# A hybrid decoder layer on one core: another order of the opening loads, the key norm behind the values, the 32×32 inverse spread over partitions, output rows in bonus tiles

## The chip, the cores and the metric

One core of a Trainium2 chip runs the whole layer. The metric is the device time of a run in microseconds; lower is better. The engines are called as in the profile: PE (TensorE), DVE (VectorE), ACT (ScalarE), POOL (GpSimd) and SP (SyncE, which here only issues DMAs).

## The reference

One layer with three branches on x of 2048 tokens by 1024 channels, in float32, beside a memory of 256 tokens:

```
h   = rms_norm(x, g);  parts of h @ w_in feed the branches and their gates
A   = RWKV-7 time mixing, 8 heads of 64 (per head a 64x64 state, delta rule)
B   = sliding-window attention, 8 query and 2 key heads of 64, window 128, sinks
kv  = rms_norm(mem, gm) @ w_mem_kv;  km = rms_norm(kv[:, :512] per head);  vm = kv[:, 512:]
C   = softmax(rms_norm(q) km') vm, 4 heads of 128 over 256 memory tokens
out = x + (sum over branches of sigmoid(gate) * ((branch * silu(z)) @ w_proj)) @ w_out
```

In chunks of 64 tokens the delta rule of branch A needs, per head and chunk, the inverse of a unit triangular 64×64 matrix.

## The kernel before

The tokens go in four blocks of 512 (`TB`; `sb` is the block). All activations are kept transposed, channels on partitions. A float32 product is made of three `float32r` matmuls on split operands, high·high, high·low and low·high (`gemm3`, L501 to L507). Every weight is split into a high and a low part: ACT copies (L487), DVE subtracts (L488). In block 0 this is done on arrival, and the split pair is stored to DRAM (`k…`, L491); blocks 1 to 3 load the pair back as one 512 KB tile `whl` (L483). `whl` has six buffers, the raw weights `raw` three.

**The opening** (L383 to L423, L1353 on). The SP queue carries the loads in the order in which they are listed: transposed memory `memt` (four tiles `g`) and key weights `w_mk` (four tiles `big`), the identity, memory rows (`yl`), rows of x (`rt`, `g`), value weights `w_mv` (four `big` tiles; the last two stand behind x's columns), x's columns `in_xt` (`ya`, `yh`). `mem_split` makes the two parts of the normed memory (tiles `mB`). `mem_kv` (L638) then makes for each of four heads the keys (24 matmuls of 256 columns; weights split at L476 and L477), their sums of squares, the pow on POOL, two transposes that spread the scale over partitions, the scaled and split key, and its store to DRAM (`Kd`). Values follow (48 matmuls of 512 columns, L684 to L686) into two PSUM banks, `oo` and `as_`. The row scales of the memory (`mem_scales`) come first of all. `x_scales` and `x_cols` (L1338) then make block 0's input `hT` (`hH`, `hL`; L1347 to L1350) from x's rows and columns, and the first projection starts.

**A block.** Two streams are woven: branch A (`stream_r`) and branches C and B with their projections (`stream_f`). In branch A, `rwkv_prep` (L735) makes for a pair of heads the tiles QE, QO, AB, BK, and copies the 32×32 diagonal pieces of AB into `Nc` on ACT (L819 to L821). After two pairs, `rwkv_inverse` (L853) inverts all 64 pieces (4 partition groups × 16) at once: 32 partitions hold one piece's rows. In step s of 31, a stream shuffle on DVE (L863) spreads row s of every piece to its 32 partitions, a multiply (L864) and an add (L865) update the columns behind s of all of `Y`, 128 partitions × 16·(31−s) columns. Then a transposition on DVE (L868) and two groups of small PE products (L880, L888) make the lower left quarter of the 64×64 inverse, and `put` stores the result to DRAM (`fb`), from where `rwkv_chain` loads it. There are two inverses per block, eight in all. Carried columns of the token shift are copied at L714.

**The end of a block.** Branch A's last projection merges into the accumulators, and `output` (L1294) multiplies by `w_out`, in two halves of 512 channels: 96 matmuls into four PSUM banks (two of `mm`, two of `as_`), and then for each of the four row tiles a buffer of the pool `g` (L1306), its load of x's rows, the add on DVE, and the store, load and store on ACT's DMA queue:

```python
                xr = g2()
                nc.scalar.dma_start(xr, A["x"][rows, n * 512:(n + 1) * 512])
                V.scalar_tensor_tensor(xr, op[tt], 0.5, xr, op0=ALU.mult, op1=ALU.add)
                nc.scalar.dma_start(A["out"][rows, n * 512:(n + 1) * 512], xr)
```

The pool `g` has 11 buffers for everything short-lived. `ya`, `yh` and `yl` have four each: `ya` holds, for each pair of heads, the bonus term and then branch A's output, until it has been split for the projection.

**The order of the work.** The program is listed in one piece and then laid out anew by a list scheduler (`Step`, `lay_out`, `order`, L55 to L314): each instruction has a cost by engine, and each engine takes the ready instruction that was listed first, as buffers allow. The result is the fixed order of each engine; at run time an engine takes its instructions in that order and waits by semaphores. A DMA is laid out with 2200 ns, one on a tensor parked in DRAM (`fq`, `fb`, `fv`) with 4200 (`cost_SP`, L142). In the names, `g_…`, `k_…` and the like are tiles with their numbers.

Of the kernel before, what the change touches and what calls it, by code (L numbers as in the profile page):

```python
# [20 lines left out]
TB = 512  # L21
# [38 lines left out]
class Step:  # L60
# [256 lines left out]
def build(tc, A, nsb=4):  # L317
# [52 lines left out]
    def const(name, shape, src=None):  # L370
        t = (bp if name == "ident" else fp if name == "eye32" else cp).tile(shape, F32, name="c_" + name)
        nc.sync.dma_start(t, A[name] if src is None else src)
        return t
# [18 lines left out]

    def mk(h):
        early(rp.tile([128, 2, 512], F32, name="big", bufs=BIG), A["w_mk"][h].rearrange("p (b c) -> p b c", b=2), raws)
# [4 lines left out]
    for u in range(2):  # L399
        early(g2(shape=(128, 2, M)), A["memt"][256 * u:256 * (u + 1)].rearrange("(k p) t -> p k t", p=128), memt)  # L400
    mk(0)
    for u in range(2, 4):
        early(g2(shape=(128, 2, M)), A["memt"][256 * u:256 * (u + 1)].rearrange("(k p) t -> p k t", p=128), memt)
    mk(1)
    ident = const("ident", [128, 128])
    for i in range(2):
        for u in range(2):
            early(yrow("yl"), A["mem"][i * 128:(i + 1) * 128, u * 512:(u + 1) * 512], mem0)
    mk(2)
    for i in range(3):  # L410
        for u in range(2):
# [6 lines left out]
    for u in range(2):  # L418
        early(g2(), A["x"][384:512, u * 512:(u + 1) * 512], x0)
    mv(0)  # L420
    mv(1)
    for k in range(8):
        early(yrow("ya" if k < 4 else "yh"), A["xt"][k * 128:(k + 1) * 128, :TB], xt0)  # L423
# [175 lines left out]
    Kd = [dp.tile([128, 2, M], F32, name=f"mk{h}") for h in range(4)]  # L599
# [38 lines left out]
    def mem_kv(mT, ms, mr):  # L638
        kgs, sts = {}, {}

        def keys(h):
            o = mm_ps()[:, :M]
            gemm3(o, [(w, (mT[0][k], mT[1][k])) for k, w in enumerate(wtiles(None, 8, raw=raws[h]))])
            sq = g2()[:, :M]
            S.activation(sq, o, AF.Square)
            kg = g2()[:, :M]
            S.activation(kg, o, AF.Copy, scale=dcol("xg"))
            kgs[h] = sq, kg

        def stats(h):  # L650
            st = s_ps()
            tok_stat(kgs[h][0], 1, 2, st)
            rs = xp.tile([128, 8], F32, name="st8", bufs=2)
            V.scalar_tensor_tensor(rs[:, :2], st[:, :2], 1.0 / 128, ms, op0=ALU.mult, op1=ALU.add)
            G.tensor_tensor(rs[:, :2], rs[:, :2], mhalf[:, :2], op=ALU.pow)
            sts[h] = rs

        def scaled(h):
            kg = kgs[h][1]
            bc = s_ps()  # L660
            bcast_T(bc, sts[h], 1, 2)
            V.tensor_tensor(kg, kg, bc[:, :M], op=ALU.mult)
            km = rp.tile([128, 2, M], F32R, name="km", bufs=2)
            S.activation(km[:, 0], kg, AF.Copy)
            V.tensor_tensor(km[:, 1], kg, km[:, 0].bitcast(F32), op=ALU.subtract)
            nc.sync.dma_start(Kd[h], km.bitcast(F32))

        o = [o_ps(), s_ps()]
        for h in range(6):
            if h < 4:  # L670
                keys(h)
                yield 3.921
            if 1 <= h < 5:
                stats(h - 1)
            if h >= 2:
                scaled(h - 2)
            yield 1.796
            if h < 4:
                continue
            for k in range(4 * h - 16, 4 * h - 12):  # L680
                wh, wl = two_parts(raws[4 + k // 2][:, k % 2])
                for i in range(2):
                    sl = slice(i * 128, (i + 1) * 128)
                    PE.matmul(o[i], mT[0][k][:, sl], wh, start=k == 0, stop=False)  # L684
                    PE.matmul(o[i], mT[0][k][:, sl], wl, start=False, stop=False)
                    PE.matmul(o[i], mT[1][k][:, sl], wh, start=False, stop=k == 7)  # L686
# [9 lines left out]
        yield 9.836  # L696
# [20 lines left out]
    def tmp(tag="rt", bufs=NRT):  # L717
        return rp.tile([128, TB], F32, name=tag, bufs=bufs)

# [15 lines left out]
    def rwkv_prep(p, i, parks, dk, Pls, Nc, sb, hT, lwla, group):  # L735
# [83 lines left out]
        for q in range(4):  # L819
            qs = slice(32 * q, 32 * q + 32)  # L820
            S.activation(Nc[qs, i], AB[qs, :, 32 * (q % 2):32 * (q % 2) + 32], AF.Copy)  # L821
# [31 lines left out]
    def rwkv_inverse(group, parks, Nc):  # L853
# [3 lines left out]
        N_ = Nc.rearrange("p i c t -> p (i c) t")  # L857
        Y = rp.tile([128, n, 32], F32, name="Yi")
        V.tensor_copy(Y, eye32.unsqueeze(1).to_broadcast([128, n, 32]))
        for s in range(31):  # L860
            w = 31 - s
            bc = rp.tile([128, n, 32], F32, name="ibc", bufs=2)
            V.stream_shuffle(bc[:, :, :w], N_[:, :, s + 1:], [s] * 32)  # L863
            V.tensor_tensor(bc[:, :, :w], bc[:, :, :w], Y[:, :, s:s + 1].to_broadcast([128, n, w]), op=ALU.mult)  # L864
# [649 lines left out]
```

## Time and profile before

| | before |
|---|---|
| median of 3 runs | 2163.45 us (2163.43 to 2164.69) |
| profiled execution | 2162.26 us |
| its span, mean granted clock | 2160.5 us, 0.998 |
| PE / DVE / ACT / POOL busy | 2132.1 / 1556.2 / 830.3 / 131.9 us |
| DMA | 511.87 MB, 237 GB/s on average |

The span is the stretch in which the profile shows instructions; the execution's own time is 1.8 us longer. Busy time of PE is that of matmuls whose ends are modelled, so 99% says that PE had matmuls under way, not at what pace: the pace is read from the distance of their starts. PE's weight loads (PEld) run beside them. A group's row gives line, engine, operation, tiles with their shapes, and count; then busy time, mean ns of one, and the idle time of that engine ahead of them with what ended it.

### The profile page before, as it was taken

What the parts mean: (1) busy time and instruction counts of PE and PEld (TensorE: products, weight loads), DVE (VectorE), ACT (ScalarE), POOL (GpSimd) and SP (SyncE); (2) the same over time, 40 slices, a digit from 0 to 9 for tenths busy, and PEclk for the clock granted to TensorE, in tenths of its full rate; (3) what the DMA queues carried; (4) which work ended last, traced back from release to release, by engine and by line L of the source; (5) the groups of instructions that cost most, each with busy time, mean ns of one, the idle gap of its engine ahead of it and who ended that gap; (6) DMA issues with size and microseconds to landing.
All of it is one profiled execution on the core that took longest, in us unless ns stands there. A gap on an engine that the chain in (4) does not pass through costs nothing.

```text
span 2160.5 us, 37816 instructions
## 1 busy us (share of the span) xinstructions
PE 2132.1 (99%) x14260; PEld 1757.0 (81%) x14260; DVE 1556.2 (72%) x3731; ACT 830.3 (38%) x1757; POOL 131.9 (6%) x159
## 2 busy tenths in 40 slices
PE   8999999999999999999999999999999999999999
PEld 6888787777788888878888888887888888887887
DVE  7799999567578979754627988955455798894532
ACT  6655554336244353303414344421522434431220
POOL 2001000001000000001000100000100000000100
PEclk9999999999999999999999999999999999999999
DMA  9988787978866566585876656676676655758556
GB/s 324 333 273 266 256 280 236 345 272 307 322 231 206 181 211 203 182 293 179 279 260 208 197 185 205 207 250 212 230 259 233 208 184 194 225 173 288 184 193 204
DMA packets 254758, 511.87 MB, mean 237 GB/s; under 512 B 38256, under 2 KB 120432, under 8 KB 254576
## 3 DMA queue, kind: packets, MB, share of 16 engines
q1 hardware_dynamic: 238448, 480.08, 66.8%
q10 hardware_dynamic: 16128, 29.37, 4.1%
q8 instruction: 113, 1.85, 0.3%
q14 instruction: 69, 0.57, 0.1%
HBM read 375.67 MB, written 133.69 MB: 236 GB/s over the span
## 4 chain that ended last, share of the span: by engine, by line
PE 82%; DVE 8%; DMA 6%; issue 1%; ACT 1%; SPq 0%; POOL 0%; ACTq 0%; DVEq 0%; POOLq 0%
PE mm L507 20%; PE mm L505 20%; PE mm L506 20%; DVE whl L488 2%; DMA rt<-in_x 1%; DMA k<-whl 1%; PE mm L1303 1%; PE mm L1301 1%; PE mm L1302 1%; PE rw L983 1%; PE rw L966 1%; PE oo L1250 1%; PE rw L806 1%; DVE ibc L863 1%; PE rw L826 1%
## 5 line engine op out<-in xcount | busy, mean ns | idle before, releaser
L505 PE MATMUL mm<-hH,whl 128*128 128x512 f32 x1888 | 746.0, 395 | 2.9 <-DVE carry L714 2.8
L506 PE MATMUL mm<-hL,whl 128*128 128x512 f32 x1888 | 743.5, 394 | 1.5 <-DVE hL L1350 1.4
L507 PE MATMUL mm<-hH,whl 128*128 128x512 f32 x1888 | 744.6, 394 | 0.0
L505 PEld LDWEIGHTS mm<-hH,whl 128*128 128x128 f32 x1888 | 355.1, 188 | 74.4 <-ACT g L1018 3.2
L506 PEld LDWEIGHTS mm<-hL,whl 128*128 128x128 f32 x1888 | 355.4, 188 | 72.2 <-DVE hL L1350 2.5
L507 PEld LDWEIGHTS mm<-hH,whl 128*128 128x128 f32 x1888 | 355.3, 188 | 70.9
L487 ACT ACTIVATE whl<-raw 128x512 fp32r<-128x512 f32 x162 | 101.6, 629 | 155.7 <-PE mm L507 105.2
L505 PE MATMUL mm<-yh,whl 128*128 128x512 f32 x384 | 151.0, 394 | 2.8 <-ACT ibc L1328 1.6
L507 PE MATMUL mm<-yh,whl 128*128 128x512 f32 x384 | 151.9, 395 | 0.0
L506 PE MATMUL mm<-yl,whl 128*128 128x512 f32 x384 | 150.7, 392 | 0.0
L488 DVE TENSOR_TENSOR whl<-raw,whl 128x512 fp32r<-128x512 f32 x162 | 111.6, 690 | 41.6 <-ACT whl L487 39.7
L863 DVE STREAM_SHUFFLE ibc<-Nc 128x496 f32<-128x496 f32 (+30 forms) x248 | 114.2, 472 | 0.0
L1269 ACT ACTIVATE gt<-mm 128x512 f32<-128x512 f32 x64 | 38.0, 594 | 190.0 <-PE mm L507 189.8
L864 DVE TENSOR_TENSOR ibc<-ibc,Yi 128x496 f32<-128x496 f32 (+30 forms) x248 | 104.5, 421 | 4.2
L865 DVE TENSOR_TENSOR Yi<-Yi,ibc 128x496 f32<-128x496 f32 (+30 forms) x248 | 103.3, 417 | 1.0
L505 PEld LDWEIGHTS mm<-yh,whl 128*128 128x128 f32 x384 | 72.1, 188 | 18.5 <-ACT ibc L1328 2.0
L506 PEld LDWEIGHTS mm<-yl,whl 128*128 128x128 f32 x384 | 72.2, 188 | 15.3 <-DVE yl L1033 0.4
L507 PEld LDWEIGHTS mm<-yh,whl 128*128 128x128 f32 x384 | 72.1, 188 | 15.3
L463 POOL TENSOR_SCALAR st<-st 128x4 f32<-128x4 f32 (+1 forms) x32 | 13.1, 409 | 1031.5 <-DVE st L1060 468.9
L1308 DVE SCALAR_TENSOR_TENSOR g<-mm,g 128x512 f32<-128x512 f32 x16 | 11.0, 690 | 88.5 <-PE mm L1303 88.5
L1284 DVE SCALAR_TENSOR_TENSOR gt<-gt,mm 128x512 f32<-128x512 f32 x32 | 22.0, 686 | 68.5 <-PE mm L507 68.1
L1218 ACT ACTIVATE g<-g,mxs,st 128x128 f32<-128x128 f32 x128 | 61.5, 484 | 18.7 <-DVE mxs L1211 18.7
(1836 smaller groups left out, 3678.5 us busy)
## 6 DMA issues: line engine op xcount, KB each, us to landing
whl<-k SPq DMA_DIRECT2D x486, 512.0 KB, 3.5
k<-whl SPq DMA_DIRECT2D x162, 512.0 KB, 4.7
raw<-in_w_in SPq DMA_DIRECT2D x118, 256.0 KB, 3.7
fq<-big SPq DMA_DIRECT2D x64, 256.0 KB, 4.3
fb<-big SPq DMA_DIRECT2D x64, 256.0 KB, 4.6
big<-fq SPq DMA_DIRECT2D x32, 512.0 KB, 6.7
big<-fb SPq DMA_DIRECT2D x32, 512.0 KB, 5.8
g<-in_x ACTq DMA_DIRECT2D x32, 256.0 KB, 4.8
```

The source lines that it names most:

```text
L487: S.activation(w[:, 0], raw, AF.Copy)
L488: V.tensor_tensor(w[:, 1], raw, w[:, 0].bitcast(F32), op=ALU.subtract)
L505: PE.matmul(out, lh, rh, start=i == 0, stop=False)
L506: PE.matmul(out, lh, rl, start=False, stop=False)
L507: PE.matmul(out, ll, rh, start=False, stop=i == n - 1)
L806: m = PE.matmul(g[:, c], BK[h, c0 + c], Q[h, c0 + c], start=True, stop=True)
L863: V.stream_shuffle(bc[:, :, :w], N_[:, :, s + 1:], [s] * 32)
L864: V.tensor_tensor(bc[:, :, :w], bc[:, :, :w], Y[:, :, s:s + 1].to_broadcast([128, n, w]), op=ALU.mult)
L865: V.tensor_tensor(Y[:, :, s + 1:], Y[:, :, s + 1:], bc[:, :, :w], op=ALU.add)
L1218: S.activation(P_, P_, AF.Exp, scale=r2[:, b, i:i + 1], bias=mx[:, b, i:i + 1], accum_out=mx[:, b, 2 + i:3 + i])
L1269: S.activation(t, gp, AF.Tanh, scale=0.5)
L1284: V.scalar_tensor_tensor(g, g, 1.0, pp, op0=ALU.add, op1=ALU.mult)
```

## The change

Three parts of the kernel change, and two details of the scheduler's table and of the constants.

*Opening.* The loads now come in this order: key weights (with `memt` between the first two), rows of x, identity, the first two tiles of value weights, x's columns, small constants, the last two tiles of value weights, memory rows last. In `mem_kv` all keys are made first and only their sums of squares kept (`sums`); the values follow, one of 8 weight rows at a time, into `oo` and `yps`; then `mem_scales`, the values' scaling and stores, and last the keys' pow (once, 8 columns) and scaling, two heads at a time. `Kd` has two tensors for two heads each.

*Inverse.* `Nc` and its ACT copies go. `rwkv_prep` writes the pieces of AB to DRAM (`fn`, four DMAs for a pair of heads, L838 of the new file). `rwkv_inverse` reads them back with one piece on each partition, twice (64 pieces on partitions 0 to 63 and again on 64 to 127; tile `Nb` in a buffer of `km`, L880). Each half of the partitions holds every other row of the solution `B`, which POOL sets to the identity (L877, L881). Step s multiplies and adds (L885, L886) on (s//2+1) × (31−s) columns, without a shuffle. `B` goes to DRAM (`fy`, two DMAs, L888) and comes back in the old layout as `Y` (four DMAs, L891), and what follows is as before. `fn` and `fy` are laid out with 4200 ns. `cross_head` takes its key and value tiles out of one larger `km` buffer, and the constant `eye32` goes.

*Output.* The row tiles of `output` take buffers of `ya`.

```diff
-        parked = any(r[0].startswith(("fq", "fb", "fv")) for r in self.reads + self.writes)
+        parked = any(r[0].startswith(("fq", "fb", "fv", "fn", "fy")) for r in self.reads + self.writes)
...
+    mt(0)
+    mk(0)
+    mt(1)
+    mt(2)
+    mt(3)
+    mk(1)
     mk(2)
-    for i in range(3):
-        for u in range(2):
-            early(rp.tile([128, TB], F32, name="rt", bufs=NRT), A["x"][i * 128:(i + 1) * 128, u * 512:(u + 1) * 512], x0)
     mk(3)
-    eye32 = const("eye32", [128, 32])
+    xrow(0)
...
+    mv(0)
+    mv(1)
+    xcol(0)
...
+    mv(2)
+    mv(3)
+    mrow(0)
+    mrow(1)
...
+        o = [o_ps(), y_ps()]
+        for h in range(4):
+            keys(h)
+            if h:
+                stats(h - 1)
+            yield
+        for k in range(8):
+            wh, wl = two_parts(raws[4 + k // 2][:, k % 2])
+            for i in range(2):
+                sl = slice(i * 128, (i + 1) * 128)
+                PE.matmul(o[i], mT[0][k][:, sl], wh, start=k == 0, stop=False)
...
+            if not k:
+                stats(3)
+            yield
+        ms, mr = mem_scales()
         for i in range(2):
             t = g2()
             S.activation(t, o[i], AF.Copy, scale=mr[:, i:i + 1])
...
+        rs = xp.tile([128, 8], F32, name="st8", bufs=2)
+        V.scalar_tensor_tensor(rs.rearrange("p (h i) -> p h i", i=2), sums, 1.0 / 128, ms.unsqueeze(1).to_broadcast([128, 4, 2]), op0=ALU.mult, op1=ALU.add)
+        G.tensor_tensor(rs, rs, mhalf[:, :8], op=ALU.pow)
+        for u, kg in enumerate(kgs):
+            bc = s_ps()
+            bcast_T(bc, rs[:, 4 * u:4 * u + 4], 1, 4)
+            V.tensor_tensor(kg, kg, bc, op=ALU.mult)
...
-            S.activation(Nc[qs, i], AB[qs, :, 32 * (q % 2):32 * (q % 2) + 32], AF.Copy)
+            nc.sync.dma_start(fn[q, i].rearrange("c s t -> s c t"), AB[32 * q:32 * q + 32, :, 32 * (q % 2):32 * (q % 2) + 32])
...
+        Nb = rp.tile([128, 32, 32], F32, name="km", bufs=2)
+        B = rp.tile([128, 16, 32], F32, name="Yi")
+        flat = B.rearrange("p a t -> p (a t)")
+        G.memset(flat, 0.0)
+        for j in range(2):
+            own = slice(64 * j, 64 * j + 64)
+            nc.sync.dma_start(Nb[own], fn.rearrange("q i c s t -> (q i c) s t"))
+            G.memset(flat[own, j:j + 511:34], 1.0)
+        for s in range(31):
+            w, m = 31 - s, s // 2 + 1
+            bc = rp.tile([128, 16, 32], F32, name="ibc", bufs=2)
+            V.tensor_tensor(bc[:, :m, :w], Nb[:, s, s + 1:].unsqueeze(1).to_broadcast([128, m, w]), B[:, :m, s:s + 1].to_broadcast([128, m, w]), op=ALU.mult)
+            V.tensor_tensor(B[:, :m, s + 1:], B[:, :m, s + 1:], bc[:, :m, :w], op=ALU.add)
+        for j in range(2):
+            nc.sync.dma_start(fy.rearrange("q i c (a j) t -> j (q i c) a t", j=2)[j], B[64 * j:64 * j + 64])
         Y = rp.tile([128, n, 32], F32, name="Yi")
-        V.tensor_copy(Y, eye32.unsqueeze(1).to_broadcast([128, n, 32]))
-        for s in range(31):
-            w = 31 - s
-            bc = rp.tile([128, n, 32], F32, name="ibc", bufs=2)
-            V.stream_shuffle(bc[:, :, :w], N_[:, :, s + 1:], [s] * 32)
-            V.tensor_tensor(bc[:, :, :w], bc[:, :, :w], Y[:, :, s:s + 1].to_broadcast([128, n, w]), op=ALU.mult)
-            V.tensor_tensor(Y[:, :, s + 1:], Y[:, :, s + 1:], bc[:, :, :w], op=ALU.add)
+        for q in range(4):
+            nc.sync.dma_start(Y[32 * q:32 * q + 32], fy[q].rearrange("i c s t -> s (i c) t"))
...
-                xr = g2()
+                xr = yrow("ya")
...
-    ms, mr = mem_scales()
-    mv(2)
-    mv(3)
-    for i, _ in enumerate(mem_kv(mT, ms, mr)):
+    for i, _ in enumerate(mem_kv(mT)):
```

The scheduler lays the whole program out anew, and since its order hangs together, much moves by a little. Three places follow, each of before and then of after.

The SP queue in the opening, before, from the identity on (ahead of it stand the four `memt` tiles and two of the key weights; `yl` are memory rows, `rt` and `g` rows of x):

```order
L372 DMA c_ident<-in_ident 128x128
L387 DMA yl<-in_mem 128x512 x4
L387 DMA big<-in_w_mk 128x1024
L387 DMA rt<-in_x 128x512 x6
L387 DMA big<-in_w_mk 128x1024
L372 DMA c_eye_145<-in_eye 128x32
L372 DMA c_bones<-in_bones 128x2
L372 DMA c_ropec<-in_ropec 128x2
L372 DMA c_sinks<-in_sinks 128x8
L387 DMA g_153<-in_x 128x512
L387 DMA g_155<-in_x 128x512
L387 DMA big<-in_w_mv 128x2x512 x2
```

And after, from the rows of x on (ahead of them stand all four key weights):

```order
L387 DMA rt<-in_x 128x512 x6
L387 DMA g_135<-in_x 128x512
L387 DMA g_137<-in_x 128x512
L372 DMA c_ident<-in_ident 128x128
L387 DMA big<-in_w_mv 128x2x512 x2
L387 DMA ya<-in_xt 128x512 x4
L387 DMA yh<-in_xt 128x512 x4
L372 DMA c_bones<-in_bones 128x2
L372 DMA c_ropec<-in_ropec 128x2
L372 DMA c_sinks<-in_sinks 128x8
L387 DMA big<-in_w_mv 128x2x512 x2
L387 DMA yl<-in_mem 128x512 x4
```

The memory rows moved from behind the second key tile to the last place, the rows of x behind all key tiles; in both, x's columns stand between the second and the third tile of value weights.

The SP queue at the first inverse of block 0. Before, the queue carries raw weights in, split weights out, and the parked tiles of branch A:

```order
L486 DMA raw<-in_w_in 128x512
L491 DMA k_2969<-whl 128x1024
L486 DMA raw<-in_w2a 128x512
L491 DMA k_2976<-whl 128x1024
L486 DMA raw<-in_w_in 128x512
L491 DMA k_3045<-whl 128x1024
L733 DMA fb_0_678<-big 128x4x128
L733 DMA fb_1_679<-big 128x4x128
```

After, the write of `fy` and the four reads of `Y` stand between them (the lines of weights and their stores are now L508 and L513):

```order
L888 DMA fy_0_659<-Yi 1024x1x32
L508 DMA raw<-in_w_in 128x512
L513 DMA k_2858<-whl 128x1024
L508 DMA raw<-in_w_in 128x512
L513 DMA k_2914<-whl 128x1024
L891 DMA Yi<-fy_0_659 32x16x32
L508 DMA raw<-in_w_in 128x512
L513 DMA k_2922<-whl 128x1024
L508 DMA raw<-in_w2a 128x512
L513 DMA k_2929<-whl 128x1024
L891 DMA Yi<-fy_0_659 32x16x32 x3
L508 DMA raw<-in_w_in 128x512
```

Between the write of `fy` and the last read of `Y` there now stand four raw loads and four stores; SP's list grew from 1181 to 1296 rows, DVE's shrank from 3146 to 2880.

ACT, with its DMA queue, at block 0's output, before, from the first half's first store on (`out<-g` are stores, `g<-in_x` loads of x's rows, ACTIVATE the weight splits):

```order
L1309 DMA out<-g_6403 128x512
L1309 DMA out<-g_6407 128x512
L487 ACTIVATE whl<-raw 128x512
L1309 DMA out<-g_6411 128x512
L1307 DMA g_6415<-in_x 128x512
L1307 DMA g_6575<-in_x 128x512
L1307 DMA g_6579<-in_x 128x512
L1309 DMA out<-g_6415 128x512
L487 ACTIVATE whl<-raw 128x512 x2
L1307 DMA g_6583<-in_x 128x512
L1307 DMA g_6587<-in_x 128x512
L1309 DMA out<-g_6575 128x512
```

After, from a weight split ahead of the first half's stores on:

```order
L509 ACTIVATE whl<-raw 128x512
L1336 DMA out<-ya 128x512 x4
L509 ACTIVATE whl<-raw 128x512
L1376 ACTIVATE hH<-rt,c_pv 128x512 x3
L509 ACTIVATE whl<-raw 128x512
L1334 DMA ya<-in_x 128x512
L509 ACTIVATE whl<-raw 128x512
L1334 DMA ya<-in_x 128x512 x3
L1336 DMA out<-ya 128x512 x4
```

Before, the load of the first half's fourth row tile (`g_6415`) stands behind the stores of the other three; after, the first half's four loads stand further up, ahead of the loads of `x_scales` (L1353), and all four loads of the second half behind the first half's four stores.

More of the change, by code (lines that the diff above doesn't have):

```diff
@@ L596, in rope @@
         V.tensor_tensor(out, u, sh, op=ALU.add)
[L599 removed]
+    Kd = [dp.tile([128, 2, 2, M], F32, name=f"mk{u}") for u in range(2)]
     Vd = dp.tile([128, 2, 512], F32, name="mv")
@@ L636, in mem_scales, with mem_kv @@
         return ms, mr
-    def mem_kv(mT, ms, mr):
-        kgs, sts = {}, {}
+    def mem_kv(mT):
+        kgs = [g2() for _ in range(2)]
+        sums = xp.tile([128, 8], F32, name="mx", bufs=2).rearrange("p (h i) -> p h i", i=2)
+        sqs = []
         def keys(h):
@@ L668, in mem_kv @@
[L668 to L673, printed above, removed]
-                stats(h - 1)
[L675 to L686, printed above, removed]
+            tok_stat(sqs[h], 1, 2, st)
```

92 lines of the change are left out of this document (44 added, 48 removed).

## The prediction

> **What bounds the kernel now.** I read the page first, then the busy time by stretches, then who made TensorE wait, then the granted clock. The page's first lines and eight stretches (columns: us, then PE, weight load, DVE, ACT, POOL busy with instruction counts, granted clock, DMA share, GB/s):
>
> ```profile
> span 2160.5 us, 37816 instructions
> PE 2132.1 (99%) x14260; PEld 1757.0 (81%) x14260; DVE 1556.2 (72%) x3731; ACT 830.3 (38%) x1757; POOL 131.9 (6%) x159
> ...
> 0.00:8.90 8.90, 5.19 (x12) 3.78 (x12) 2.75 (x18) 3.96 (x8) 1.64 (x10) 1.00 0.71 224
> 8.90:25.20 16.30, 14.29 (x100) 13.67 (x101) 12.95 (x34) 12.96 (x33) 2.87 (x4) 0.90 1.00 359
> 25.20:40.30 15.10, 13.72 (x72) 11.31 (x71) 13.38 (x29) 9.13 (x18) 6.25 (x9) 1.00 0.83 292
> 40.30:48.90 8.60, 7.11 (x29) 4.55 (x29) 8.60 (x15) 5.79 (x10) 0.69 (x1) 1.00 1.01 380
> ...
> 594.00:2106.00 1512.00, 1510.26 (x10288) 1245.76 (x10287) 1065.58 (x2628) 527.08 (x1134) 85.95 (x98) 1.00 0.66 216
> 2106.00:2160.50 54.50, 49.52 (x218) 40.35 (x216) 11.81 (x18) 1.90 (x3) 0.00 (x0) 1.00 0.61 204
> ```
>
> PE is busy 99% of the span; from 594 to 2106 us it idles 1.7 us in all. The change leaves PE's own work as it is (the program has the same 11,628 matmuls and transposes on that engine before and after), so all that can be won lies in PE's 28.4 us of idle time, of which nearly all stands before 594 us and in the last 54 us. Who ended that idle time, asked of 0 to 60, 60 to 600 and 600 us to the end (line waited for, us in total, times, longest):
>
> ```profile
> PE mm L505 <- ACT whl L476: 2.9, 2, 1.6
> ...
> PE mm L1301 <- DVE g L1308: 2.9, 1, 2.9
> PE mm L505 <- DVE carry L714: 2.8, 1, 2.8
> PE mm L505 <- ACT ibc L1328: 1.6, 1, 1.6
> PE oo L1250 <- DVE g L1238: 1.3, 2, 1.0
> ...
> PE as__22023 L1301 <- DVE g L1308: 1.3, 1, 1.3
> PE as__16912 L1301 <- DVE g L1308: 0.9, 1, 0.9
> PE as__11687 L1301 <- DVE g L1308: 0.2, 1, 0.2
> ```
>
> Three sources can be touched: the opening (the split key weights, L476, above all), the output stage (L1301 waiting for L1308), and VectorE's load in block 0 (L714, L1238). A wait of some 2 to 3 us has a second price, seen in the clock column of stretches behind the gaps:
>
> ```profile
> 10.50:13.90 3.40, 3.40 (x19) 3.40 (x18) 3.37 (x10) 2.86 (x8) 0.00 (x0) 0.50 1.05 396
> 13.90:17.30 3.40, 3.40 (x30) 3.40 (x30) 1.68 (x7) 2.19 (x6) 0.69 (x1) 1.00 1.05 400
> 266.40:269.90 3.50, 3.50 (x15) 2.90 (x14) 2.50 (x7) 0.81 (x2) 0.00 (x0) 0.51 0.99 316
> 566.80:570.20 3.40, 3.40 (x9) 2.64 (x9) 1.54 (x3) 0.63 (x1) 0.00 (x0) 0.51 1.02 381
> ```
>
> At half clock 19 matmuls took 3.40 us where 30 followed in the next 3.40 at full clock, so a slump costs 3.40 × 11/30 = 1.25 us. The 2.9 us wait for L1308 and the 2.8 us wait for L714 are the two followed by one; the 1.6 us wait isn't.
>
> **The opening.** Four edits belong together: the order of loads, the second part of the value gemm in a PSUM bank of its own, the key norm behind the values, x columns ahead of memory rows. Spacing of matmuls (first column the start in us), the time at which the third value-weight tile arrives, and VectorE's half of a split (mean ns):
>
> ```profile
> 14.11 0.29 PE L507 MATMUL mm<-mB,whl 128*128 128x256 f32 x1
> 14.23 0.28 PE L505 MATMUL mm<-mB,whl 128*128 128x256 f32 x1
> ...
> 2153.93 0.39 PE L1301 MATMUL mm<-whl,g 128*128 128x512 f32 x1
> 2154.15 0.39 PE L1302 MATMUL mm<-whl,g 128*128 128x512 f32 x1
> ...
> 33.58 1.16 ACT L476 ACTIVATE whl<-big 128x512 fp32r<-128x512 f32 x2 [1.93 <-DMA big<-in_w_mv]
> ...
> L477 DVE TENSOR_TENSOR whl<-big,whl 128x512 fp32r<-128x512 f32 x10 | 6.6, 689 | 3.0 <-ACT whl L476 3.0
> ```
>
> A matmul of 256 columns costs 0.12 us, one of 512 columns 0.22 to 0.23 (0.227 below). The first key weights come one 0.262 MB load earlier, 0.7 us at 359 GB/s: PE starts at about 8.2 instead of 8.9. The key stage lasted 16.3 us; without the wait for the fourth key tile (the 1.6 of the 2.9) it takes 14.7, slump included, and ends near 22.9. The first half of the values is 24 × 0.227 = 5.4 us plus some 0.4 us of transposes: 28.7. The third value tile landed at 33.5 in before, behind the memory rows (1.05 MB); these now stand behind it, which at some 330 GB/s (between the 292 and 359 above) is 3.2 us: 30.3, and with half of the 1.16 us ACT pair and a VectorE subtraction of 0.69 it is usable at 31.6. So a new wait of about 2.9 us stands in the middle of the values, as long as those that a slump followed: 1.25 us more. The second half ends at 31.6 + 5.4 + 1.25 = 38.3, against 40.3 before; but before had by then done six of the key norm's eight transposes (0.7 us, an estimate at 0.12 each as for 256 columns), so 1.3 us are won. Behind it, PE lost about 2.4 us in 40.3 to 48.9 (26 × 0.227 plus two transposes is 6.2 of 8.6), with VectorE busy 8.60 of 8.60; VectorE now gets the columns while PE waits, and I take half of that back: 1.2. Opening: −2.5 us. Bounds: 0, if the later mem sums and key products crowd VectorE as before; −6.65 if neither the new wait nor its slump comes (2.5 + 2.9 + 1.25). The key's DRAM round trip now ends later, but PE's first use of it is also 11 us of matmuls later in its order, so it costs nothing unless the memory rows land over 10 us late. Removing the row `c_eye` (16 KB) is free.
>
> [...]
>
> **Output rows in bonus tiles.** The stall has its cause in the row loads; VectorE's longest wait between 520 and 600 us,
>
> ```profile
> DVE g L1308 <- DMA g<-in_x: 7.0, 1, 7.0
> ```
>
> and the issue list gives load and store (issues, KB each, us to landing):
>
> ```profile
> g<-in_x ACTq DMA_DIRECT2D x32, 256.0 KB, 4.8
> out<-g ACTq DMA_DIRECT2D x32, 256.0 KB, 4.9
> ```
>
> The fourth row tile of each half found no free buffer in the pool `g`, its load was issued late, L1308 waited 7.0 us for it, and PE for the bank. Four `ya` tiles are free once the branch has been split, and the order puts all four loads ahead of the stage. That removes 2.9 + 1.25 (slump) + 1.3 + 0.9 + 0.2 = 6.55 us. The second half's loads now wait on ACT's queue for the first half's stores; behind them there stand in block 0 the last weight splits. Store and load take some 4.9 + 4.8 us, and the half has 96 × 0.227 = 21.8 us of matmuls, so it is covered; uncovered it would cost what it does now. The next block's bonus tile waits for these stores as well, tens of us before it is written. I take −5.5, bounds −6.55 and −2.
>
> **The inverse by partitions.** Removed on VectorE, and the smallest shape for the law of its cost:
>
> ```profile
> L863 DVE STREAM_SHUFFLE ibc<-Nc 128x496 f32<-128x496 f32 (+30 forms) x248 | 114.2, 472 | 0.0
> L864 DVE TENSOR_TENSOR ibc<-ibc,Yi 128x496 f32<-128x496 f32 (+30 forms) x248 | 104.5, 421 | 4.2
> L865 DVE TENSOR_TENSOR Yi<-Yi,ibc 128x496 f32<-128x496 f32 (+30 forms) x248 | 103.3, 417 | 1.0
> ...
> L864 DVE TENSOR_TENSOR ibc<-ibc,Yi 128x16 f32<-128x16 f32 x1 | 0.2, 179 | 0.0
> ```
>
> 322 us go, 40.3 per inverse. The 31 widths average 256 columns at 421 ns against 179 at 16, so a column costs about 1.0 ns and an instruction 0.163 us. The new loop has 31 × 2 instructions and (31−s)·(s//2+1) columns in step s, 2856 in all: 2 × (31 × 0.163 + 2.86) = 15.8 us per inverse, 126 in all. VectorE is relieved of 24 us per inverse, and ACT of the 64 small copies into `Nc`, but after 594 us PE hardly waits for either. What counts is block 0: 2.8 + 1.25 + 1.3 = 5.4 us of waits for VectorE (L714 with its slump, L1238), neither inside the loop itself. I take half, −2.7, bounds 0 and −5.4.
>
> Against this stand four serial DRAM hops per inverse and some 16 DMAs more on SP's queue. Nearest rows (issues, KB each, us to landing) and what SP waits for:
>
> ```profile
> whl<-k SPq DMA_DIRECT2D x486, 512.0 KB, 3.5
> fv<-rt SPq DMA_DIRECT2D x64, 64.0 KB, 3.7
> Zt<-fv SPq DMA_DIRECT2D x64, 64.0 KB, 4.5
> ...
> SPq L483 <- PE mm L507: 911.6, 382, 5.7
> ...
> q1 hardware_dynamic: 238448, 480.08, 66.8%
> ```
>
> The hops come to some 4 × 4.5 = 18 us, beside PE's other projections. Queued behind the waiting read on SP are weight loads; six `whl` tiles of 12 matmuls hold 16 us of PE's work, and SP waits 911.6 us for PE to free them, so a hold under 10 us is invisible. PE, which takes its instructions in order, waits where the inverse's matmuls come up before Y has landed; 27 VectorE rows stand between the last step and the transposition of Y. Bounds: 0 and 8 × 2.5 us (a slump included). With waits that the new interleaving makes elsewhere I take +2.5. The memsets that build the identity go to POOL, busy 6% of the span, long ahead of the loop: nothing.
>
> **Sum.** −2.5 − 5.5 − 2.7 + 2.5 = −8.2 on the profiled execution's 2162.26 us (span 2160.5 and 1.8 around it), 2154.1. The median of the runs shown is 1.2 above that execution, so I forecast 2155.0.
>
> **The rivals.** (1) No change: the opening stays bound by its bytes, which are the same 10 MB, and the new order brings as many waits as it removes. For it: three of the removed waits are coincidences of a laid-out order, and this one is laid out anew. 2161, chance 0.14; 0.2% (4.3 us) is about what a measurement of this kernel can tell from no change. (2) Slower: Y lands after PE has come to the inverse's matmuls. The gains without my +2.5 are 10.7 us, so the kernel is 4.3 us slower from 15/8 = 1.9 us lost per inverse. At a wait of 1.8 us with a slump behind each, 8 × 3.05 = 24.4, less 10.7: 2177; at half of the inverses 12.2, or 2165. Against it: the order leaves VectorE rows in between, and in the wait list PE never waits at the two present matmul groups. Chance 0.10. (3) Small runs clog the engines: 6144 pieces of 128 bytes per inverse. By the q1 row a packet takes 66.8% × 2160.5 × 16 / 238448 = 97 ns for 2 KB on average; at that price 37 us of all engines per inverse, in a stage that stands at two thirds already: over some 80 us 0.66 + 0.46 is 0.12 or 10 us too much, eight times, less 10.7: 2233. By bytes it is 6 ns, 2.4 us, nothing. `fv<-rt` has runs of 256 bytes and lands like the 512 KB load, so I hold to the low end. Chance 0.04. [...] (4) Better: no new wait at all, 2146, chance 0.10.
>
> **How the numbers follow.** Forecast 0.62, the rivals 0.14, 0.10, 0.04, 0.10. Below 2159.1 lie 0.57 of the forecast's share, all of rival 4 and 0.03 of rival 1; within 0.2% 0.05 of the forecast, 0.11 of rival 1 and 0.01 of rival 2; the rest is slower: faster 0.70, same 0.17, slower 0.13. The range leaves out rival 3, the larger half of rival 2 and the deepest part of rival 4, and reaches from 2145 to 2167.
>
> **What would show it.** Right: the 594-to-2106 stretch still full; no wait at L1328 (the old L1301) and no slump at 567; hT's first matmul near 38 us with one wait for split value weights near 30; shuffles gone, DVE near 1360 us. Wrong: PE waits behind the transposed Y or SP holds of 10 us at the reads of fn and fy; a DMA share up by more than 0.05; a new slump inside a block.

## The result and the profile after

The changed kernel takes 2150.29 us (median of 6 runs, 2147.60 to 2152.94), the kernel before 2163.44 (6 runs, 2159.72 to 2166.14): a ratio of 0.9942, with a 95% interval of 0.9931 to 0.9954, or 12.5 us less (10 to 15). The forecast was 2155.0 with a range of 2145 to 2167. The profiled execution of the changed kernel took 2150.37 us, and its span is 11.9 us shorter than before. The page's first lines, and stretches cut like those of before (start and end, length, then PE, weight load, DVE, ACT, POOL busy, granted clock, DMA share, GB/s):

```profile
span 2148.6 us, 37415 instructions
PE 2130.0 (99%) x14260; PEld 1752.3 (82%) x14260; DVE 1411.7 (66%) x3222; ACT 800.1 (37%) x1691; POOL 138.9 (6%) x180
```

```profile
0.00:7.05 7.05, 4.68 (x12) 3.71 (x13) 2.73 (x18) 3.94 (x7) 2.39 (x13) 1.00 0.69 224
7.05:20.90 13.85, 13.34 (x108) 12.92 (x106) 10.66 (x27) 11.18 (x28) 1.21 (x2) 1.00 1.05 392
20.90:29.10 8.20, 6.99 (x35) 5.30 (x34) 5.62 (x13) 5.31 (x11) 0.00 (x0) 1.00 1.00 325
29.10:35.40 6.30, 5.86 (x25) 4.54 (x25) 6.30 (x11) 4.63 (x10) 0.22 (x1) 1.00 0.81 302
...
594.00:2100.00 1506.00, 1505.11 (x10260) 1240.37 (x10259) 956.07 (x2247) 500.33 (x1080) 89.86 (x113) 1.00 0.71 221
```

PE starts at 7.05 instead of 8.9 us, the key stage takes 13.85 instead of 16.3, and the clock is 1.00 in every stretch. The long middle is as full as it was. What ended PE's idle time, in 0 to 60, 60 to 600 and 600 us to the end (us in total, times, longest):

```profile
PE oo L688 <- ACT whl L498: 0.9, 1, 0.9
PE mm L527 <- ACT whl L498: 0.5, 1, 0.5
PE oo L689 <- DVE whl L499: 0.4, 1, 0.4
...
PE mm L1328 <- DVE g L1311: 1.5, 2, 1.0
PE mm L527 <- DVE carry L735: 1.4, 1, 1.4
PE mm L527 <- DVE gt L1311: 1.2, 1, 1.2
...
PE as__6354 L1328 <- DVE ya L1335: 0.8, 1, 0.8
...
PE mm L1328 <- DVE ya L1335: 0.5, 1, 0.5
...
PE mm L1328 <- DVE g L1311: 0.4, 1, 0.4
```

The 2.9 us wait for the row tile (then L1308, now L1335) has become 0.8 and 0.5; those in the blocks behind are gone; the 2.8 us wait for the carried column is 1.4. Behind the wait of 2.4 us at the very start, which both kernels have, no wait is above 1.4 us, and no stretch at half clock is left in this execution, where there were three (granted clock 0.50 to 0.51). The first matmul of block 0's first projection, before and then after (start in us, duration):

```profile
40.34 0.39 PE L505 MATMUL mm<-hH,whl 128*128 128x512 f32 x1
```

```profile
35.40 0.39 PE L527 MATMUL mm<-hH,whl 128*128 128x512 f32 x1
```

So 4.9 of the 11.9 us are won ahead of block 0, and 7 behind it.

### The profile page after: what moved, and what is told of

Its sections match the earlier page's. It is cut to its first block, busy times and chain, and to the rows that moved or that the text cites. A ratio compares the mean times of both kernels' runs of the same rounds, so it can differ in the third digit from the quotient of the medians.

```text
span 2148.6 us, 37415 instructions
## 1 busy us (share of the span) xinstructions
PE 2130.0 (99%) x14260; PEld 1752.3 (82%) x14260; DVE 1411.7 (66%) x3222; ACT 800.1 (37%) x1691; POOL 138.9 (6%) x180
## 3 DMA queue, kind: packets, MB, share of 16 engines
q1 hardware_dynamic: 292288, 490.56, 70.8%
## 4 chain that ended last, share of the span: by engine, by line
PE 72%; DVE 1%; DMA 1%; ACT 1%; POOL 0%; issue 0%; ACTq 0%; POOLq 0%
PE mm L527 18%; PE mm L528 18%; PE mm L529 18%; PE mm L1328 1%; PE mm L1329 1%; PE mm L1330 1%; PE oo L1277 1%; PE rw L1009 1%; PE rw L992 1%; PE rw L824 1%; DMA raw<-in_w_out 1%; PE rw L843 0%; PE oo L824 0%; DMA rt<-in_xt 0%; DMA rt<-in_x 0%; PE rw L914 0%
## 5 line engine op out<-in xcount | busy, mean ns | idle before, releaser
L528 PEld LDWEIGHTS mm<-hL,whl 128*128 128x128 f32 x1888 | 355.0, 188 | 70.1 <-DVE hL L1377 0.6
L1335 DVE SCALAR_TENSOR_TENSOR ya<-mm,ya 128x512 f32<-128x512 f32 x16 | 11.1, 691 | 109.4 <-PE mm L1330 109.4
L885 DVE TENSOR_TENSOR ibc<-km,Yi 128x126 f32<-128x126 f32 (+22 forms) x248 | 63.0, 254 | 6.3 <-DMA km<-fn 0.7
L886 DVE TENSOR_TENSOR Yi<-Yi,ibc 128x126 f32<-128x126 f32 (+22 forms) x248 | 62.7, 253 | 5.0
L489 POOL TENSOR_TENSOR st<-st,mhalf 128x8 f32<-128x8 f32 (+1 forms) x36 | 53.6, 1490 | 3.0
```

The source lines that it names most:

```text
L489: G.tensor_tensor(out, out, mhalf[:, :n], op=ALU.pow)
L528: PE.matmul(out, lh, rl, start=False, stop=False)
L885: V.tensor_tensor(bc[:, :m, :w], Nb[:, s, s + 1:].unsqueeze(1).to_broadcast([128, m, w]), B[:, :m, s:s + 1].to_broadcast([128, m, w]), op= ...
L886: V.tensor_tensor(B[:, :m, s + 1:], B[:, :m, s + 1:], bc[:, :m, :w], op=ALU.add)
```

## The experiments

**The parts, alone and taken out: eight kernels.** The change has three parts that can be told apart: the opening (O), the inverse with its DRAM round trip (I), and the output's row tiles (Y). Six kernels complete the set. The first three have one part alone; their diffs against before are the change's own pieces, with the memory's keys in tiles of one head where the old inverse stands. That of Y:

```diff
-                xr = g2()
+                xr = yrow("ya")
```

The opening alone:

> The kernel before with the new opening alone. Theory (each part has its own worth, as the two traces put it): block 0's first projection starts about 35.4 us instead of 40.3, and 5 us stay to the end: 2158.4. By the prediction's size for this term (-2.5): 2161. Rival (the gain behind the opening is one of the order laid out anew, so that every version has stalls of its own in block 0): the first projection still starts 5 us earlier, but the total lies anywhere from 2155 to 2163, with stalls at places that neither kernel had.

The output's row tiles alone:

> The kernel before with the output's row tiles in the bonus tiles alone. Theory: the 3.0 us wait for the row tile in block 0's output with its 1.25 us at half clock goes, and the waits of 0.2, 0.9 and 1.3 us in the blocks behind: 6 us less what comes late next there, 1 to 3 us as in the changed kernel: 2158 to 2160. By the prediction's term (-5.5): 2158. Rival (order): the stalls only move, 2163 plus or minus 2.

The inverse alone; its one line that is not the change's own:

```diff
-            km = rp.tile([128, 2, M], F32R, name="km", bufs=2)
+            km = rp.tile([128, 4, M], F32R, name="km", bufs=2)[:, :2]
```

> The kernel before with the inverse by partitions alone. Theory: VectorE's load falls by 145 us as in the changed kernel (1556 to about 1411), the 2.8 us wait for the carried column and its stretch at half clock shrink: 2159, that is 4 to 5 us won. By the prediction (-2.7 + 2.5): 2163. Rival (order): stalls of its own, 2158 to 2166. PE does not wait at the inverse's two groups of products in any of these.

The other three are the changed kernel with one part taken back. Without Y (the diff above reversed):

> The changed kernel with the output's row tiles in the pool g again. Theory: the wait for a late row tile comes back in at least one block's output, 2 to 4 us: 2152 to 2154. By the prediction's term: 5.5 us more, 2156. Rival (the row tiles were a coincidence of the old order and do not come back): 2150, no difference.

Without O:

> The changed kernel with the old opening. Alone, the three parts gave 3.3, 6.7 and 3.4 us by their ratios, 13.4 together, and the whole change 12.5. Theory A (the parts add): 3 to 4 us of the gain go, 2153.5. Theory B (the opening's 5 us head start is kept to the end only where the rest of block 0 has slack, so it is worth more beside the other two parts than alone): 5 us go, 2155.5.

Without I, where the keys are again stored by head:

```diff
-            km = rp.tile([128, 2, 2, M], F32R, name="km", bufs=2)
...
+            for j in range(2):
+                km = rp.tile([128, 2, M], F32R, name="km", bufs=2)
+                kj = kg[:, j * M:(j + 1) * M]
+                S.activation(km[:, 0], kj, AF.Copy)
+                V.tensor_tensor(km[:, 1], kj, km[:, 0].bitcast(F32), op=ALU.subtract)
+                nc.sync.dma_start(Kd[2 * u + j], km.bitcast(F32))
```

> The changed kernel with the old inverse (the keys scaled in tiles of one head each, since the tile for two heads is the new inverse's). Theory A (the parts add): 2153.5. Theory B (VectorE's relief is what lets the opening's head start through): 2156 or more, with PE again losing 2 to 5 us more than the changed kernel between 60 and 260 us.

Measured, with the profiled execution cut at two marks: the first matmul on `hH`, and the last matmul of block 0's output. "Us" is the ratio less 1, times 2163.44; each ratio is to the kernel before measured beside it. What taking a part out costs is a difference of two such ratios, and uncertain by some 3.5 us (an estimate from the two intervals).

| parts | ratio to before (95%) | us | to block 0 | block 0 | behind it |
|---|---|---|---|---|---|
| none (before) | 1 | 0 | 40.3 | 549.5 | 1570.6 |
| O | 0.9985 (0.9976 to 0.9993) | -3.2 | 34.8 | 554.4 | 1573.8 |
| Y | 0.9969 (0.9957 to 0.9981) | -6.7 | 40.4 | 546.0 | 1568.6 |
| I | 0.9984 (0.9975 to 0.9994) | -3.5 | 42.2 | 540.7 | 1575.6 |
| O, Y | 0.9975 (0.9966 to 0.9984) | -5.4 | 34.5 | 550.6 | 1568.5 |
| I, Y | 0.9972 (0.9961 to 0.9983) | -6.1 | 40.9 | 544.9 | 1570.3 |
| O, I | 0.9962 (0.9950 to 0.9974) | -8.2 | 35.4 | 541.3 | 1574.2 |
| O, I, Y (after) | 0.9942 (0.9931 to 0.9954) | -12.5 | 35.4 | 543.7 | 1569.5 |

The stretches are of single executions, and executions of one kernel lie 5 us and more apart (the kernel before 2159.72 to 2166.14), so what all four pairs show counts most. The opening brings block 0 forward by 5.5, 5.9, 5.5 and 6.8 us. In the two pairs with the old inverse block 0 gives it back (+4.9 and +4.6 us), in the two with the new one it does not (-1.2 and +0.6). The first of these rests on the slowest of O's 12 executions (2164.75 us, the median 2159.89), and by its ratio O alone keeps 3.2 us of the 5.5; the second agrees with its ratios, by which O beside Y wins nothing. The new inverse shortens block 0 in every pair (8.8, 13.1, 6.9 and 1.1 us). The row tiles shorten what lies behind block 0 in every pair (2.0, 5.3, 5.3, 4.7). So the parts do not simply add: O beside Y wins nothing that can be told (-5.4 against -6.7), and beside I and Y it wins 6.5 us. That O and I together win more than their sum (8.2 against 6.7) lies within the intervals. Taken out of the whole, O costs 6.5 us, I 7.1 and Y 4.3.

Against the expectations: O alone lies where the theory of an order with stalls of its own had it, Y alone wins more than any theory said, and I alone is near the 2159 of its theory. Without Y the prediction's term (2156) was closer than the theory. Without O and without I the times came as the theories B had them (2155.5, and 2156 or more), and without I the waits too: PE idles 4.7 us from 60 to 260, and in the changed kernel 0.7. That VectorE's relief is the cause, as that theory has it, is not shown by this.

Where the head start goes, in that execution of the kernel with the opening alone: who made PE wait from 60 to 600 us.

```profile
PE mm L528 <- ACT gt L1289: 3.6, 3, 1.5
PE as__5974 L568 <- DVE rt L566: 2.2, 1, 2.2
PE mm L528 <- DVE gt L1039: 2.0, 1, 2.0
PE as__2008 L542 <- ACT g L1153: 1.6, 1, 1.6
...
PE as__1643 L542 <- ACT g L1072: 1.2, 1, 1.2
```

Its stretches from 60 and from 180 us, the same of the changed kernel, and the second of the kernel before:

```profile
60.00:180.00 120.00, 115.18 (x620) 95.94 (x619) 100.80 (x205) 68.44 (x145) 11.76 (x13) 0.99 0.84 284
180.00:260.00 80.00, 79.02 (x565) 65.87 (x565) 78.74 (x209) 44.41 (x94) 6.60 (x9) 1.00 0.78 264
```

```profile
60.00:180.00 120.00, 119.49 (x647) 99.83 (x646) 97.71 (x190) 68.60 (x142) 13.10 (x16) 1.00 0.88 296
180.00:260.00 80.00, 79.83 (x575) 66.79 (x575) 68.65 (x176) 45.50 (x107) 6.05 (x9) 1.00 0.83 272
```

```profile
180.00:260.00 80.00, 79.02 (x568) 65.93 (x567) 78.23 (x216) 47.82 (x111) 6.85 (x9) 1.00 0.79 267
```

PE idles 4.8 us from 60 to 180 against 0.5, in three waits for VectorE and ScalarE (2.0, 1.6 and 1.2 us), and a stretch at half clock follows one of them (granted clock 0.50 from 167.3 to 170.7 us). There the head start is lost. The kernel with O and Y shows it too: it idles 3.5 us there, in the same three places, and the kernel before 0.1. The second stretch does not count: the kernel before, too, idles 1.0 us in it.

Why PE waits in the first stretch is not settled. VectorE is about as busy in it as in the kernel before, which does not wait there (100.8 and 102.6 of 120 us; the changed kernel 97.7). The wait of 2.0 us, at 82.9 us, lies far ahead of the old loop's first step at 144. At the 1.6 us wait, which ended at 165.1 us while the old loop was running, ScalarE had itself waited 4.7 us for VectorE. So the order of the instructions has a part in it, VectorE's load may have one, and no run parts the two.

**Where the row tiles pay.** In the kernel with O and I but not Y, PE's waits from 600 us on:

```profile
PE as__21837 L1328 <- DVE g L1335: 1.3, 1, 1.3
PE as__16766 L1328 <- DVE g L1335: 1.2, 1, 1.2
...
PE as__11581 L1328 <- DVE g L1335: 0.6, 1, 0.6
```

These three are gone in the changed kernel. The next kernel uses the bonus tiles in blocks 1 to 3 alone.

```diff
-                xr = yrow("ya")
+                xr = yrow("ya") if sb else g2()
```

> The changed kernel with the output's row tiles in the pool g again in block 0, and in the bonus tiles in blocks 1 to 3; the order differs from the changed kernel's in a few dozen rows only. The eight versions with and without each part say that beside the new inverse the bonus tiles cost some 2 to 4 us in block 0 and win 4.5 to 5 behind it. By that: 2147 to 2148. Rival (block 0's row tiles come late again as in the kernel before, 2.9 us and 1.25 at half clock): 2153 to 2155. Each is a difference between single executions that scatter by 2 us, so 2150 is the third answer: nothing.

2149.60 us (2149.16 to 2150.28), ratio 0.9940 (0.9927 to 0.9952): the changed kernel's time. So beside the two other parts the row tiles in block 0 are worth nothing that can be told either way, the 2 to 4 us read off the table were scatter, and Y's 4.3 us lie in blocks 1 to 3. In this kernel, with `g` in block 0, the old stall doesn't return, and PE's waits there (500 to 600 us) are of another kind:

```profile
PE mm L1328 <- DVE g L1311: 2.2, 1, 2.2
PE mm L1328 <- DVE g L1335: 0.5, 1, 0.5
```

**The loads' order in the opening.** The memory rows go back behind the second key weights.

```diff
     mk(1)
+    mrow(0)
+    mrow(1)
     mk(2)
...
     mv(3)
-    mrow(0)
-    mrow(1)
```

> The changed kernel with the memory rows behind the second key weights, where they stood before, and nothing else moved in the text. By the prediction's working the third tile of value weights then comes 3.2 us later (1.05 MB at 330 GB/s): the wait for it grows from 1.0 to about 4 us with a stretch at half clock behind it, block 0's first projection starts near 40 us instead of 35.4, and the end is 4 us later: 2154. Rival (the opening is bound by VectorE rather than by its loads, and the sums done early make up for it): the first projection within 1.5 us of 35.4, 2150 to 2151.

2156.98 us (2156.40 to 2159.17), ratio 0.9974 (0.9964 to 0.9985): 6.9 us of the gain go. The first projection, and PE's waits in 0 to 60 us:

```profile
39.06 0.39 PE L527 MATMUL mm<-hH,whl 128*128 128x512 f32 x1
```

```profile
PE oo L688 <- ACT whl L498: 1.9, 2, 1.0
PE mm L527 <- ACT hH L1376: 1.5, 1, 1.5
```

PE's waits are shorter than the 4 us expected; its matmuls ran at half clock (0.50 granted) from 23.6 to 27.0 us instead. 39.06 was forecast as near 40; the rival (VectorE bounds the opening) falls. The place of the memory rows alone carries 3.7 of the opening's 4.9 us; the other 3.2 of the 6.9 us are lost behind the first projection, and by what was not asked.

**VectorE's load put back.** Each multiplication of the new loop three times.

```diff
-            V.tensor_tensor(bc[:, :m, :w], ..., op=ALU.mult)
+            for _ in range(3):
+                V.tensor_tensor(bc[:, :m, :w], ..., op=ALU.mult)
```

> The changed kernel with each multiplication of the new inverse done three times (the same product into the same tile), so that VectorE is at about 1412 + 126 = 1538 us, near the 1556 of before, and each loop takes some 16 us longer, while the traffic through DRAM stays. If VectorE's relief is what the inverse's part gives: 3 to 4 us slower than the changed kernel, 2153.5 to 2154.5. If it is the order laid out anew that gives it, or the waits behind the loop: 2150, plus or minus 2.

2268.96 us (2268.55 to 2273.70), ratio 1.0502 (1.0486 to 1.0518). Neither theory had this: VectorE is busy 1523 us, less than before, and the kernel is 5% slower. Who waited, VectorE first, then PE, then the third transposition in the timeline:

```profile
DVE ibc L895 <- DMA Yi<-fy: 30.1, 8, 8.2
```

```profile
PE rw L824 <- DVE big L813: 32.3, 4, 8.8
PE oo L1278 <- DVE big L832: 19.0, 4, 4.8
```

```profile
826.37 0.71 DVE L895 STREAM_TRANSPOSE ibc<-Yi 128x512 f32<-128x512 f32 x1 [8.18 <-DMA Yi<-fy]
```

With the longer loop the order leaves too little between the loop and the transposition: VectorE waits for Y to come back from DRAM, 8.2 us at the worst, and behind it in VectorE's order stands the preparation of the next pair, for which PE waits up to 8.8 us. It is the prediction's second rival one engine further up. The two rows of PE are 51 of the 86 us by which its idle time grew (from 18.6 to 105.0 us); the other 32 of the 118 us by which the span grew are PE's own busy time (2161.8 us against 2130.0), at a granted clock of 0.976 on average instead of 1.000. The run doesn't tell what load alone costs, since the loop's length changed the order too.

**The price of the small pieces.** First every small write twice, laid out by the scheduler.

```diff
-            nc.sync.dma_start(fn[q, i].rearrange("c s t -> s c t"), AB[...])
+            for f in (fn, fn2):
+                nc.sync.dma_start(f[q, i].rearrange("c s t -> s c t"), AB[...])
...
-            nc.sync.dma_start(fy.rearrange(...)[j], B[64 * j:64 * j + 64])
+            for f in (fy, fy2):
+                nc.sync.dma_start(f.rearrange(...)[j], B[64 * j:64 * j + 64])
```

> The changed kernel with every write of small pieces made twice: the 32x32 pieces into fn and the solution into fy each go a second time to a tensor that nobody reads. That adds 4096 pieces of 128 bytes per inverse, 32768 in all, two thirds as many again as the change brought. By the count of packets between the two profiles (53837 more packets for 4 points of q1's share, some 23 ns each over 16 engines): 32768 x 23 ns / 16 = 47 us of the engines' 2150, 2 points of share, and no time: 2150 to 2152. By the rival of the small runs (97 ns a packet): 9 points of share, and several us where block 0 stands at 0.9: 2155 or more.

2161.05 us (11 executions, 2157.10 to 2162.22 and one of 12093.91, in which what happened was not recorded), ratio 0.9993 (0.9984 to 1.0002), as the small pieces' rival had it; but the order of every engine had changed with it. So the same writes, each behind its first in an otherwise unchanged order:

```diff
+    todo, extra, prev = [], {}, None
+    for ins in tc.nc.cur_bb.bb.instructions:
+        if isinstance(ins, mybir.InstDMA) and any(a.bass_ap.tensor.name.startswith(("fnx", "fyx")) for a in ins.outs):
+            extra[prev.name] = ins
...
+        l = [i for s in l for i in (s.ins, extra.get(s.ins.name)) if i is not None]
```

> The changed kernel with every write into fn and fy made a second time, in the same small pieces, to a tensor that nobody reads; unlike the doubled writes before, each second write stands right behind its first and the order of every engine is the changed kernel's own, so that SP's list has 80 DMAs more and nothing else differs. If the 10 us of the doubled writes came from the order that was laid out anew: 2150 to 2152. If they came from 32768 more pieces of 128 bytes: 2157 to 2161.

And the same 80 DMAs and bytes in long pieces:

```diff
-                nc.sync.dma_start(f[q, i].rearrange("c s t -> s c t"), AB[32 * q:32 * q + 32, :, 32 * (q % 2):32 * (q % 2) + 32])
+            nc.sync.dma_start(fn2[q, i].rearrange("c (s u) t -> (c s) (u t)", u=8), AB[32 * q:32 * q + 32, 6:8].rearrange("p c t -> p (c t)"))
...
-                nc.sync.dma_start(f.rearrange("q i c (a j) t -> j (q i c) a t", j=2)[j], B[64 * j:64 * j + 64])
+            nc.sync.dma_start(fy2.rearrange("q i c (j a) t -> j (q i c) (a t)", j=2)[j], B[64 * j:64 * j + 64].rearrange("p a t -> p (a t)"))
```

> As the run before, the same order and the same 80 DMAs with the same bytes out of the same tiles, but in pieces of 1 and 2 KB instead of 128 bytes. By both theories the changed kernel's time and what 80 more DMAs on SP's queue cost: 2150 to 2152. The difference to the run before is the price of small pieces alone: nothing by the order theory, 7 to 10 us by the small pieces.

Small pieces: 2156.60 us (2155.92 to 2157.17), ratio 0.9973 (0.9962 to 0.9984). Long pieces: 2153.84 (2152.59 to 2156.37), 0.9962 (0.9949 to 0.9974). Both theories miss. 80 more DMAs in long pieces cost 4.3 us against the changed kernel; the pieces' size adds 2.4, within the intervals, and not 7 to 10. Of the 11 us that the first version lost (0.9993 less 0.9942), 4.3 (0.9993 less 0.9973) are the order's alone. What the engines paid, small and then long (queue, packets, MB, share of 16 engines):

```profile
q1 hardware_dynamic: 326336, 494.76, 71.1%
```

```profile
q1 hardware_dynamic: 296640, 494.76, 70.1%
```

29,696 packets more for (71.1% × 2154.9 - 70.1% × 2154.3) × 16 = 352 us: 12 ns each, not 97. How DMAs on SP's queue reach PE is seen at block 0's second inverse: VectorE's wait for the pieces (first in the changed kernel, from its waits of 300 to 400 us; then in the run with long pieces, from the timeline, with PE's wait out of 260 to 541 us).

```profile
DVE ibc L885 <- DMA km<-fn: 0.7, 1, 0.7
```

```profile
333.08 0.19 DVE L894 TENSOR_TENSOR ibc<-km,Yi 128x31 f32<-128x31 f32 x1 [2.90 <-DMA km<-fn]
```

```profile
PE as__3975 L1236 <- DVE g L1242: 1.9, 1, 1.9
```

The loop's first multiplication waits for the read of `fn` behind more DMAs (its second half is issued at 327.00 us instead of 325.67); the attention's masking (L1242) stands behind it on VectorE, and PE waits for that. That is 1.9 of the 4.3 us; the rest was not traced, nor whether the second writes also hold their source tiles longer.

## Why the prediction was right, point by point

**Direction and size.** Faster, by 12.5 us (10 to 15) against 8.4. Two terms were too small, and the third came near only as a sum, with its parts in other places; that it did is luck. Of the signs, the long middle stayed full (0.9 us idle of 1506) and the slump at 567 is gone; the waits at L1328 shrank to 0.8 and 0.5 us for the row tiles instead of going, and the first projection came at 35.4 us and not near 38.

**The opening, -2.5 forecast.** It was worth about twice as much and more: 4.9 us in the profile at the first projection, 6.5 (0.9972 less 0.9942) when taken out. The mechanism held: the place of the memory rows' bytes decides, and moving them back moved the first projection to 39.06, near the 40 that follows from the prediction's rate. Three sizes were off. The start: 8.9 to 7.05 is 1.9 and not 0.7. The first key tile, before and then after, with ScalarE's wait for it:

```profile
8.24 1.15 ACT L476 ACTIVATE whl<-big 128x512 fp32r<-128x512 f32 x2 [2.42 <-DMA big<-in_w_mk]
```

```profile
5.61 1.15 ACT L498 ACTIVATE whl<-big 128x512 fp32r<-128x512 f32 x2 [0.59 <-DMA big<-in_w_mk]
```

Its load is issued 0.5 us earlier (1.65 instead of 2.14), and it is there 2.6 us earlier. One load of 0.262 MB less ahead of it does not explain that: even at the 224 GB/s of the whole first stretch it is 1.2 us. Why the load itself took less time is open. The key stage took 13.85 and not 14.7, with no slump, at 392 GB/s and not the old 359. The wait for the third value tile was 0.9 and 0.4 us, not 2.9 with 1.25 at half clock, since the tile was split from 28.43 on:

```profile
28.43 1.15 ACT L498 ACTIVATE whl<-big 128x512 fp32r<-128x512 f32 x2 [0.35 <-DMA big<-in_w_mv]
```

The forecast had it usable at 31.6. What the prediction did not ask is whether block 0 lets a head start through. Beside Y and the old inverse it doesn't, beside Y and the new one it does; O alone keeps 3.2 us.

**Output rows, -5.5 forecast.** Alone 6.7 us (4.1 to 9.3), near the forecast. Taken out of the whole, 4.3, in blocks 1 to 3, where the prediction had put 2.4 and had 4.15 in block 0. The step that failed is that block 0's late row tile would stay a wait without the edit: in the new order it costs 0.5 us from `g` too. The rival "no change" was right so far that this stall was a matter of the order.

**The inverse, -2.7 with +2.5 against it.** The new loop's cost was right: 126 us forecast,

```profile
L885 DVE TENSOR_TENSOR ibc<-km,Yi 128x126 f32<-128x126 f32 (+22 forms) x248 | 63.0, 254 | 6.3 <-DMA km<-fn 0.7
L886 DVE TENSOR_TENSOR Yi<-Yi,ibc 128x126 f32<-128x126 f32 (+22 forms) x248 | 62.7, 253 | 5.0
```

125.7 measured. VectorE's total fell by 144.5 us, not by the 196 between the group rows. Neighbouring instructions overlap in the records, and a group's row counts each in full: taken together, the old loop's records cover 295 us, and 248 of VectorE's 1556 without overlap with any other instruction. "Near 1360" was wrong for the most part for that reason. The net was forecast at -0.2 us and came out at -3.5 alone and -7.1 beside the other two, with block 0 shorter in every pair. At the inverse's products, where the +2.5 has its main cause, PE waits for nothing that comes of the inverse, so that term was too large; whether the relief, half of 5.4 us, was too small as well is not known, since the run that put VectorE's load back did not settle it. The round trip's length was priced well. Four hops (issues, KB each, us to landing),

```profile
km<-fn SPq DMA_DIRECT2D x16, 256.0 KB, 4.9
fn<-big SPq DMA_DIRECT2D x64, 32.0 KB, 3.8
fy<-Yi SPq DMA_DIRECT2D x16, 128.0 KB, 4.3
Yi<-fy SPq DMA_DIRECT2D x32, 64.0 KB, 3.6
```

16.6 us against 18. The cover is thin, as 80 more DMAs and the longer loop showed.

**The rivals.** Slower by a late Y did not come in this order; the longer loop shows its path through VectorE. Clogging by small pieces did not come: q1's share rose from 66.8% to 70.8% for 53,840 more packets, and in the second writes, in pieces of 128 bytes instead of 1 and 2 KB, each packet more cost 12 ns of engine time (an estimate from q1's two shares, 71.1% and 70.1%). The granted clock halved after waits of 2.8 and 2.9 us, as the prediction had read it. But the length of a wait did not decide it: in the kernel with the opening alone a wait of 1.6 us was followed by half clock, and the prediction had a wait of 1.6 us as harmless. More on this below.

## What to carry to other kernels

A head start ahead of a stage is worth what that stage lets through: look for the waits of the stage behind, since the same edit won nothing beside one set of other edits and 6.5 us beside another. When a scheduler lays the program out anew, a term that rests on one coincidence of its order, such as a late buffer, has to be asked again of the new order. To price an added DMA or instruction in such a program, add it to the frozen order: laid out anew, the same 80 DMAs cost 4 us more.

## What the runs showed of the hardware

The kernel before ran at a granted clock of 0.50 to 0.51 in three stretches of 3.4 us, from 10.5, 266.4 and 566.8 us on. The last two began 1.2 and 0.2 us after the waits of 2.8 and 2.9 us had ended, the first 1.6 us after one of 1.35 us (at 8.92 us) and behind another of 0.22. So a wait of 1.6 us can be followed by half clock and cost the 1.25 us more of the prediction's estimate, as in the kernel with the opening alone, where it ended at 165.1 us,

```profile
163.90:167.30 3.40, 2.16 (x14) 1.95 (x15) 3.40 (x10) 2.03 (x5) 0.11 (x1) 1.00 0.91 307
167.30:170.70 3.40, 3.40 (x10) 2.63 (x8) 3.40 (x7) 0.36 (x1) 2.24 (x2) 0.50 0.69 230
```

and a wait of 1.36 us need not, as in the changed kernel, where it ended at 264.9 us:

```profile
262.30:265.70 3.40, 2.04 (x10) 1.40 (x9) 3.31 (x8) 0.63 (x1) 0.00 (x0) 1.00 0.63 149
265.70:269.10 3.40, 3.40 (x70) 2.86 (x69) 2.73 (x5) 0.68 (x2) 0.00 (x0) 1.00 1.06 375
```

The length of a wait alone does not tell whether half clock follows; what does, these runs do not show.
